# A hybrid decoder layer: where the last stage's weights are split, and how the S5 tables and the S5 scan are spread

## The chip, the core and the metric

The kernel runs on one core of a Trainium2 chip, in one launch. The metric is the device time in microseconds (us) from start to end. The core has a matrix engine (TensorE, PE in the profile; the loads of its stationary operand are PEld), three engines for elementwise work (VectorE = DVE, ScalarE = ACT, GpSimd = POOL) and SyncE (SP), which here issues the DMAs. Each engine works off its own instructions in the order in which the program holds them, and waits on semaphores for the others.

## The reference, cut to what matters

One layer over 2048 tokens of width 1024, in float32:

```
h = rms_norm(x);  proj = h @ w_in                        # 1024 -> 8716 columns
u_a, z_a, q, k, v, z_b, xbc, dt, z_c, gate_logits = split(proj)
y_a = s5_mixer(u_a, ...) * silu(z_a)                     # 32 diagonal complex state spaces, then a GLU
y_b = attention_mixer(q, k, v) * silu(z_b)               # 12 heads, windows (128,1) (512,4) (2048,16)
y_c = ssd_mixer(xbc, dt, z_c, ...)                       # conv, chunked scan, gated norm
g0, g1, g2 = sigmoid(gate_logits)
merged = g0 * (y_a @ proj_a) + g1 * (y_b @ proj_b) + g2 * (y_c @ proj_c)
out = x + merged @ w_out
```

Two pieces of it do not depend on x: the tables of the S5 scan (powers and phases of its complex decays, its B and C matrices multiplied out), and the weights proj_a, proj_b, proj_c and w_out themselves.

## The kernel before

Each large product is made of three matmuls: both operands are split into a high part and the rest (hi, lo; in code `wh`, `wl`), and hi*hi, hi*lo and lo*hi are added up. So every weight is first copied by ACT to its high part and then subtracted by DVE to its low part.

The main line is the input projection, in two halves of 1024 tokens. For each half the columns are taken in groups of 256, and a group takes four units. The first half's order is q, k, v and z_b of the attention (units 1 to 40), dt and z_c (41 to 52), xbc (53 to 72), u_a and z_a, called uz (73 to 88), and the gates (89 to 136); the second half's is uz (137 to 152), q, k, v (153 to 192), dt and z_c, xbc, gates (to 272). For each group `wload` brings 1 MB of weights into one buffer (`wr`), and `wsplit` (L361) splits it in four quarters (L368 on ACT, L369 on DVE); there are six buffers for high and six for low quarters, so that two quarters of the next group are split early and the other two only when TensorE has left the first quarters of the present one. TensorE's results stand in three PSUM banks (`mmps`) and are taken out by ACT.

Beside the main line run jobs, written as generators. `main` gives each a number of steps and a first and last unit between which its steps are spread evenly; what a step emits is then ordered on each engine by a scheduler that works with its own estimates before the program ever runs, so that a job's instructions often stand ahead of the unit in which they were emitted. The jobs that matter here:

- `s5_setup` (units 2 to 38) makes small S5 values, nearly all on DVE.
- `s5_tables` (40 steps): for each of eight blocks, products on POOL (L1060, L1061, L1104, L1105), adds on DVE, four transposes and four small matmuls on TensorE, and stores.
- `ssd` for the first half's chunks: decay matrices on POOL (L814) and matmuls on TensorE.
- `a0_early` (8 steps) norms the eight token tiles 8 to 15 of the second half: ACT squares, POOL takes the inverse root of the mean (L245, L246; tile `xs`), DVE multiplies x (L289), and TensorE transposes it (L295, tile `xT`).
- `out_weights` (20 steps) reads proj_a, proj_b, proj_c and w_out, splits them and stores them for the last stage (`pw_d`, `wo_d`). A step is one slab of 128 x 1024: a load into `ow`, ACT's copy (L1240) and DVE's subtraction (L1241) into `owh`, and two stores. Both tiles have two buffers.
- `s5` (42 steps) is the scan, `s5_glu` (25 steps) what follows it; then the second half's attention, its scan, and `final`, the last stage.

All DMAs named here stand in SP's one queue. Jobs take their tiles from pools that are opened and closed one after the other in the same memory.

Of the kernel before, what the change touches and what calls it, by code (L numbers as in the profile page):

```python
# [10 lines left out]
F32 = mybir.dt.float32  # L11
F32R = mybir.dt.float32r
BF16 = mybir.dt.bfloat16
I32 = mybir.dt.int32
AF = mybir.ActivationFunctionType
ALU = mybir.AluOpType
# [4 lines left out]
D = 1024  # L21
P = 128
# [5 lines left out]
NEG = -1.0e30  # L28
TABW = 162
ATTEND = 256  # L30
S5END = 196


class Small:
# [115 lines left out]
class Hybrid:  # L150
# [1074 lines left out]
    def out_weights(self):  # L1225

        nc, A = self.nc, self.A
        for j in range(20):
            if j < 4:
                src, k, scale = A["proj_a"], j, 0.125  # L1230
            elif j < 6:
                src, k, scale = A["proj_b"], j - 4, 0.5
            elif j < 12:
                src, k, scale = A["proj_c"], j - 6, self.snw[:, j - 6:j - 5]
            else:
                src, k, scale = A["w_out"], j - 12, 0.5
            raw = self.ct(f"ow{j}", [P, D], tag="ow", bufs=2)
            nc.sync.dma_start(raw, src[0, k * P:(k + 1) * P, :])
            hl = self.ct(f"owh{j}", [P, 2, D], F32R, tag="owh", bufs=2)
            nc.scalar.activation(hl[:, 0], raw, AF.Copy, scale=scale)  # L1240
            nc.vector.scalar_tensor_tensor(hl[:, 1], raw, scale, hl[:, 0].bitcast(F32),  # L1241
                                           op0=ALU.mult, op1=ALU.subtract)
            for x in range(2):
                if j < 12:
                    dst = self.pw_d[:, :, x, j, :].rearrange("t p c -> p t c")
                    nc.sync.dma_start(dst, hl[:, x].bitcast(F32).rearrange("p (t c) -> p t c", c=P))
                else:
                    dst = self.wo_d[:, :, x, j - 12, :].rearrange("t p c -> p t c")
                    nc.sync.dma_start(dst, hl[:, x].bitcast(F32).rearrange("p (t c) -> p t c", c=256))
            yield  # L1250

    def load_y(self, tb):
# [89 lines left out]
    def main(self):  # L1342
# [6 lines left out]
        def early(gen, n):  # L1349
            for _ in range(n):  # L1350
                yield next(gen)
# [20 lines left out]
        def open_pool(name):  # L1372
            st = ExitStack()
            return st, st.enter_context(self.tc.tile_pool(name=name, bufs=1, side="right"))

        def run(jobs, until):

            nonlocal u
            adv = steps(jobs)
            while u < until:  # L1380
                if next(units, 0) is None:
                    u += 1
                    adv(u)
                else:
                    break
            adv(10 ** 6)
# [9 lines left out]

        u, units = 0, all_units()
        st, self.jp = open_pool("jp0")
        run([(self.s5_setup(), 18, 2, 38)], 40)
        st.close()  # L1400
        s1, self.sp = open_pool("sp0")
        s2, self.jp = open_pool("jp1")
        ssd0, early0 = self.ssd(0), self.a0_early()
        run([(early(ssd0, 10), 10, 73, 82), (chain(self.attention(0, 0), self.attention(1, 0)), 40, 41, 80)], 82)
        s2.close()
        s2, self.jp = open_pool("jp1t")
        run([(early(ssd0, 36), 36, 83, 116), (self.s5_tables(), 40, 83, 115), (early0, 8, 84, 115)], 116)
        s2.close()
        s2, self.jp = open_pool("jp1w")
        run([(ssd0, 20, 117, 135), (self.out_weights(), 20, 117, 134)], 136)  # L1410
        s2.close()
        s1.close()
        st, self.jp = open_pool("jp2")
        run([(self.s5(), 42, 153, 180)], 180)
        st.close()
        st, self.jp = open_pool("jp2g")
        run([(self.s5_glu(), 25, 181, S5END)], S5END)
        st.close()
        self.late = [None, None]
        self.late[0], self.sp = open_pool("sp1")  # L1420
# [58 lines left out]
```

## Time and profile before

| | |
|---|---|
| median of 3 runs | 2519.76 us (2518.63 to 2520.58) |
| the profiled execution | 2518.61 us, its span 2516.5 us |
| TensorE busy | 2453.7 us, 98% of the span |
| VectorE, ScalarE, GpSimd busy | 1336.7, 783.9, 708.7 us |
| mean granted clock of TensorE | 0.986 |

The span is the time from the first to the last instruction; 2.1 us of the execution lie outside it. A matmul's row in the profile is longer than the time until the next one starts, since matmuls overlap; TensorE counts as busy while any of them runs. The clock is given as a share of the full 2.4 GHz, and it has two levels here, 1.00 and 0.50.

### The profile page before, as it was taken

To read this page: it belongs to the slowest core of one execution; us is meant where nothing else is said; L and a number is where in the kernel's file an instruction comes from. 1 tells how busy PE (TensorE), PEld (TensorE's weight loads), DVE (VectorE), ACT (ScalarE), POOL (GpSimd) and SP (SyncE) were. 2 spreads that over 40 slices of the span, in tenths; PEclk is the share of its full clock that TensorE was granted. 3 is DMA by queue.
4 is the path that set the end of the run, shared out by engine and by line. 5 is a ranking of instruction groups with operands and counts; after the bars stand their busy time and mean duration, and the time that the engine had idled before them with its cause. 6 is when DMAs were issued, how large, how long until landed. Compare 5 with 4: busy or idle time off the path is not lost.

```text
span 2516.5 us, 40172 instructions
## 1 busy us (share of the span) xinstructions
PE 2453.7 (98%) x15216; PEld 2158.3 (86%) x15216; DVE 1336.7 (53%) x2852; ACT 783.9 (31%) x1656; POOL 708.7 (28%) x737
## 2 busy tenths in 40 slices
PE   8999999999999999999999999999999899999999
PEld 8999988887777888899999988888887688888888
DVE  6942545538666443277765545632334767563321
ACT  4222344432223434222244244533332312121100
POOL 2221000029887330054442000000111455432120
PEclk8999999999999999999999999999999999999999
DMA  7433333435555997556554333433333789887886
GB/s 169 128 107 98 104 103 101 154 87 181 176 181 178 335 355 233 139 144 173 174 165 152 127 106 92 148 124 128 112 126 112 227 303 308 290 286 264 306 290 223
DMA packets 417088, 453.41 MB, mean 180 GB/s; under 512 B 103040, under 2 KB 358272, under 8 KB 409728
## 3 DMA queue, kind: packets, MB, share of 16 engines
q1 hardware_dynamic: 416896, 450.86, 56.2%
q8 instruction: 120, 1.97, 0.3%
q14 instruction: 72, 0.59, 0.1%
HBM read 304.80 MB, written 145.97 MB: 179 GB/s over the span
## 4 chain that ended last, share of the span: by engine, by line
PE 55%; DMA 6%; DVE 5%; POOL 4%; SPq 2%; issue 1%; ACT 1%; DVEq 0%; ACTq 0%; POOLq 0%
PE ps_g L392 5%; PE ps_g L394 5%; PE ps_g L393 5%; PE fp L1300 3%; PE fp L1302 3%; PE fp L1301 3%; PE op L1333 2%; PE op L1331 2%; PE op L1332 2%; PE ao L688 2%; PE ps_xbc L393 2%; PE ps_xbc L394 1%; PE ps_xbc L392 1%; PE as L659 1%; PE ps_uz L394 1%
## 5 line engine op out<-in xcount | busy, mean ns | idle before, releaser
L392 PE MATMUL ps_g<-hT_hi,wh_g 128*128 128x512 f32 x768 | 308.8, 402 | 1.6 <-DVE e_uz L466 1.1
L393 PE MATMUL ps_g<-hT_lo,wh_g 128*128 128x512 f32 x768 | 306.7, 399 | 0.0
L394 PE MATMUL ps_g<-hT_hi,wl_g 128*128 128x512 f32 x768 | 306.0, 398 | 0.0
L814 POOL TENSOR_TENSOR sr<-tle,ahl 128x384 fp32r<-128x384 f32 x128 | 122.1, 977 | 440.0 <-PE sd L819 305.9
L392 PEld LDWEIGHTS ps_g<-hT_hi,wh_g 128*128 128x128 f32 x768 | 144.8, 188 | 35.2 <-DVE e_uz L466 2.0
L394 PEld LDWEIGHTS ps_g<-hT_hi,wl_g 128*128 128x128 f32 x768 | 144.9, 189 | 33.5 <-issue 0.5
L393 PEld LDWEIGHTS ps_g<-hT_lo,wh_g 128*128 128x128 f32 x768 | 145.0, 189 | 32.7 <-issue 1.0
L1300 PE MATMUL fp<-fy_hi,fp 128*128 128x512 f32 x384 | 154.3, 402 | 0.5 <-DVE fg L1303 0.5
L1333 PE MATMUL op<-fo,fm_lo 128*128 128x256 f32 x512 | 146.3, 287 | 7.2 <-DVE fm_lo L1313 7.2
L1331 PE MATMUL op<-fo,fm_hi 128*128 128x256 f32 x512 | 147.8, 289 | 4.9 <-DMA fo<-wo_d 2.8
L1302 PE MATMUL fp<-fy_hi,fp 128*128 128x512 f32 x384 | 151.3, 394 | 0.0
L1301 PE MATMUL fp<-fy_lo,fp 128*128 128x512 f32 x384 | 150.9, 393 | 0.0
L1332 PE MATMUL op<-fo,fm_hi 128*128 128x256 f32 x512 | 146.5, 286 | 0.0
L1305 POOL TENSOR_TENSOR fm<-fm,fg 128x512 f32<-128x512 f32 x64 | 85.5, 1336 | 206.6 <-DVE fg L1303 190.9
L667 ACT ACTIVATE sm<-sm,ml 128x256 f32<-128x256 f32 (+1 forms) x192 | 86.4, 451 | 137.9 <-DVE ml L665 111.1
L392 PE MATMUL ps_xbc<-hT_hi,wh_xbc 128*128 128x512 f32 x320 | 129.0, 403 | 0.0
L394 PE MATMUL ps_xbc<-hT_hi,wl_xbc 128*128 128x512 f32 x320 | 128.6, 402 | 0.0
L393 PE MATMUL ps_xbc<-hT_lo,wh_xbc 128*128 128x512 f32 x320 | 128.6, 402 | 0.0
L369 DVE TENSOR_TENSOR wl_g<-wr_g,wh_g 128x512 fp32r<-128x512 f32 x96 | 77.2, 826 | 92.2 <-ACT wh_g L368 91.9
L506 DVE SCALAR_TENSOR_TENSOR ac_cv<-xb_cv,convw,ac_cv 128x512 f32<-128x512 f32 x120 | 91.6, 764 | 49.1 <-ACT ac_cv L504 48.3
L383 PE MATMUL ps_q<-wh_q,hT_lo 128*128 128x256 f32 x384 | 109.9, 287 | 3.0 <-DVE hT_lo L325 3.0
L381 PE MATMUL ps_q<-wh_q,hT_hi 128*128 128x256 f32 x384 | 111.2, 291 | 0.3 <-ACT wh_q L368 0.3
(418 smaller groups left out, 6953.8 us busy)
## 6 DMA issues: line engine op xcount, KB each, us to landing
fp<-pw_d SPq DMA_DIRECT2D x32, 1536.0 KB, 6.8
fo<-wo_d SPq DMA_DIRECT2D x16, 2048.0 KB, 8.7
wr_g<-in_w_in_dram SPq DMA_DIRECT2D x24, 1024.0 KB, 5.4
g_d<-e_g SPq DMA_DIRECT2D x96, 256.0 KB, 2.9
fg<-g_d SPq DMA_DIRECT2D x96, 256.0 KB, 7.0
pw_d<-owh SPq DMA_DIRECT2D x24, 512.0 KB, 6.5
wr_xbc<-in_w_in_dram SPq DMA_DIRECT2D x10, 1024.0 KB, 5.4
x<-in_x_dram SPq DMA_DIRECT2D x32, 256.0 KB, 4.4
```

What stands on the lines that cost most here:

```text
L381: nc.tensor.matmul(ps, hi[:, t], wh, start=kt == 0, stop=False)
L383: nc.tensor.matmul(ps, lo[:, t], wh, start=False, stop=kt == KT - 1)
L392: nc.tensor.matmul(ps, wh, hi, start=kt == 0, stop=False)
L393: nc.tensor.matmul(ps, wh, lo, start=False, stop=False)
L394: nc.tensor.matmul(ps, wl, hi, start=False, stop=kt == KT - 1)
L814: nc.gpsimd.tensor_mul(r, self.tle.unsqueeze(1).to_broadcast([P, 3, P]), ahl[:, i, h0:h0 + 3].unsqueeze(2).to_broadcast([P, 3, P]))
L1300: nc.tensor.matmul(ps, W[k][0], yh[k], start=k == k0, stop=False)
L1301: nc.tensor.matmul(ps, W[k][0], yl[k], start=False, stop=False)
L1302: nc.tensor.matmul(ps, W[k][1], yh[k], start=False, stop=k == k1 - 1)
L1331: nc.tensor.matmul(ps, mh[k][:, t], W[k][0], start=k == 0, stop=False)
L1332: nc.tensor.matmul(ps, mh[k][:, t], W[k][1], start=False, stop=False)
L1333: nc.tensor.matmul(ps, mlo[k][:, t], W[k][0], start=False, stop=k == 7)
```

## The change

Three lines of numbers in `main` and one generator change.

- `out_weights` runs in units 23 to 40, in the pool of `s5_setup`, and no longer in the last third of the first half's gates. It handles each slab in two halves of 512 columns: two loads of 256 KB, two copies, two subtractions and four stores of 256 KB where there were one load, one copy, one subtraction and two stores, all of twice the size. Both tiles keep two buffers, now of half the size. The stores still put 512 bytes in a row for `pw_d` and 1 KB for `wo_d`.
- `s5_tables` has its 40 steps in units 83 to 135 where they had 83 to 115, and the 56 steps of `ssd` that remain run evenly through 83 to 135, where 36 ran to 116 and 20 from 117. One pool (`jp1t`) holds until unit 136, and `jp1w` is gone.
- `s5` gets units 153 to 184 for its 42 steps where it had 153 to 180, `s5_glu` 185 to 200 for 181 to 196, and the second half's attention begins at 202 for 198 and ends as before.

```diff
-S5END = 196
+S5END = 200
...
-            raw = self.ct(f"ow{j}", [P, D], tag="ow", bufs=2)
-            nc.sync.dma_start(raw, src[0, k * P:(k + 1) * P, :])
-            hl = self.ct(f"owh{j}", [P, 2, D], F32R, tag="owh", bufs=2)
...
+            for q in range(2):
+                raw = self.ct(f"ow{j}_{q}", [P, 512], tag="ow", bufs=2)
+                nc.sync.dma_start(raw, src[0, k * P:(k + 1) * P, q * 512:q * 512 + 512])
+                hl = self.ct(f"owh{j}_{q}", [P, 2, 512], F32R, tag="owh", bufs=2)
+                nc.scalar.activation(hl[:, 0], raw, AF.Copy, scale=scale)
+                nc.vector.scalar_tensor_tensor(hl[:, 1], raw, scale, hl[:, 0].bitcast(F32),
+                                               op0=ALU.mult, op1=ALU.subtract)
...
-        run([(self.s5_setup(), 18, 2, 38)], 40)
+        run([(self.s5_setup(), 18, 2, 38), (self.out_weights(), 20, 23, 40)], 40)
...
-        run([(early(ssd0, 36), 36, 83, 116), (self.s5_tables(), 40, 83, 115), (early0, 8, 84, 115)], 116)
-        s2.close()
-        s2, self.jp = open_pool("jp1w")
-        run([(ssd0, 20, 117, 135), (self.out_weights(), 20, 117, 134)], 136)
+        run([(ssd0, 56, 83, 135), (self.s5_tables(), 40, 83, 135), (early0, 8, 84, 115)], 136)
...
-        run([(self.s5(), 42, 153, 180)], 180)
+        run([(self.s5(), 42, 153, 184)], 184)
...
-        run([(self.s5_glu(), 25, 181, S5END)], S5END)
+        run([(self.s5_glu(), 25, 185, S5END)], S5END)
```

What the scheduler makes of it is seen in the built order of the instructions. On GpSimd, just ahead of the inverse root of the early token tile 10 (`xs10`, the third of the eight), before; `s5...` are products of the tables, `sx`, `sxd`, `sxdd`, `sr` and `ssd_state` belong to the scan of branch C:

```order
L836 TENSOR_TENSOR sx1_6646<-sx1_6646,sy1_1_7104 128x384
L1105 TENSOR_TENSOR s5wt3_1_7732<-s5t3_7497 128x512
L795 TENSOR_TENSOR sxd2_7213<-sx2_7203,dt0_5988 128x768
L1105 TENSOR_TENSOR s5wt3_1_7732<-s5t3_7497 128x512
L796 TENSOR_TENSOR sx2_7203<-sx2_7203,hpar_423 128x768
L798 TENSOR_TENSOR sxdd2_7216<-sxd2_7213,edc0_6119 128x768
L245 TENSOR_SCALAR sss1_7150<-sss1_7150 128x1
L246 TENSOR_TENSOR sss1_7150<-sss1_7150,nhalf_104 128x1
L1060 TENSOR_TENSOR s5k3_7512<-s5t3_7497 128x512
L1060 TENSOR_TENSOR s5o3_7605<-s5t3_7497 128x512
L245 TENSOR_SCALAR xs10_7260<-xs10_7260 128x1
L246 TENSOR_TENSOR xs10_7260<-xs10_7260,nhalf_104 128x1
```

And at the same place now:

```order
L843 TENSOR_TENSOR ssd_state_422<-ssd_state_422,edc0_6399 128x384
L836 TENSOR_TENSOR sx1_6926<-sx1_6926,sy1_1_7345 128x384
L1060 TENSOR_TENSOR s5k2_7873<-s5t2_7795 128x512
L795 TENSOR_TENSOR sxd2_7469<-sx2_7459,dt0_6268 128x768
L796 TENSOR_TENSOR sx2_7459<-sx2_7459,hpar_423 128x768
L798 TENSOR_TENSOR sxdd2_7472<-sxd2_7469,edc0_6399 128x768
L245 TENSOR_SCALAR sss1_7397<-sss1_7397 128x1
L246 TENSOR_TENSOR sss1_7397<-sss1_7397,nhalf_104 128x1
L245 TENSOR_SCALAR xs10_7483<-xs10_7483 128x1
L246 TENSOR_TENSOR xs10_7483<-xs10_7483,nhalf_104 128x1
```

The tables are in their third block there (the names end in 2) where they were at the end of the fourth.

On ScalarE in the first half's q, k, v stretch, where the third and fourth quarters of the second k group (`wh_k1`) are copied, before; `e_...` are results taken out of PSUM and `sq_...` their squares:

```order
L432 COPY e_q1_0_1_1539<-ps_q1_0_1_1490 128x512
L434 ACTIVATE sq_q1_0_1_1540<-e_q1_0_1_1539 128x512
L432 COPY e_q1_1_0_1622<-ps_q1_1_0_1573 128x512
L434 ACTIVATE sq_q1_1_0_1623<-e_q1_1_0_1622 128x512
L368 CAST wh_k1_0_2_1790<-wr_k1_0_1780 128x2x256
L368 CAST wh_k1_0_3_1794<-wr_k1_0_1780 128x2x256
L432 COPY e_q1_1_1_1681<-ps_q1_1_1_1632 128x512
```

And now:

```order
L432 COPY e_q1_0_1_1539<-ps_q1_0_1_1490 128x512
L434 ACTIVATE sq_q1_0_1_1540<-e_q1_0_1_1539 128x512
L1241 ACTIVATE owh8_0_2913<-ow8_0_2911,snw_430 128x512
L1241 ACTIVATE owh8_1_2920<-ow8_1_2918,snw_430 128x512
L432 COPY e_q1_1_0_1622<-ps_q1_1_0_1573 128x512
L434 ACTIVATE sq_q1_1_0_1623<-e_q1_1_0_1622 128x512
L1241 ACTIVATE owh9_0_2995<-ow9_0_2993,snw_430 128x512
L368 CAST wh_k1_0_2_1790<-wr_k1_0_1780 128x2x256
L1241 ACTIVATE owh9_1_3002<-ow9_1_3000,snw_430 128x512
L368 CAST wh_k1_0_3_1794<-wr_k1_0_1780 128x2x256
L432 COPY e_q1_1_1_1681<-ps_q1_1_1_1632 128x512
```

Copies of the last stage's weights stand between the main line's, one of them between two quarters of k. The 40 of them begin in the third unit and end ahead of the result of the 30th.

## Rows read from the trace of the kernel before

**Rows 1.** Stretches: length, busy PE PEld DVE ACT POOL, clock, DMA share, GB/s

```profile
60.00:255.00 195.00, 195.00 (x1653) 195.00 (x1652) 105.69 (x448) 53.84 (x91) 41.51 (x40) 1.00 0.37 111
...
560.00:820.00 260.00, 242.11 (x1123) 192.95 (x1122) 180.10 (x212) 75.67 (x160) 225.43 (x198) 0.95 0.55 176
820.00:976.50 156.50, 156.50 (x731) 128.03 (x730) 75.26 (x94) 63.94 (x102) 47.08 (x46) 1.00 0.98 319
976.50:1066.00 89.50, 89.50 (x391) 72.58 (x390) 23.88 (x32) 28.37 (x42) 0.13 (x2) 1.00 0.63 175
1066.00:1384.00 318.00, 308.56 (x2400) 301.17 (x2399) 219.50 (x352) 104.38 (x185) 126.20 (x149) 0.99 0.55 163
```

**Rows 2.** PE's waits, 560 to 820: total us, times, longest

```profile
PE xT L295 <- DVE x L289: 14.9, 7, 4.6
```

**Rows 3.** Timeline, PE: start us, us, instruction, idle before it and releaser

```profile
603.89 2.29 PE L295 MATMUL xT<-ident,x 128*128 128x128 f32 x8 [4.62 <-DVE x L289]
...
634.10 1.12 PE L295 MATMUL xT<-ident,x 128*128 128x128 f32 x4 [3.46 <-DVE x L289]
...
700.27 0.66 PE L295 MATMUL xT<-ident,x 128*128 128x128 f32 x4 [2.84 <-DVE x L289]
...
764.92 0.66 PE L295 MATMUL xT<-ident,x 128*128 128x128 f32 x4 [2.60 <-DVE x L289]
```

**Rows 4.** Timeline of GpSimd ahead of the first of these waits

```profile
597.67 2.11 POOL L245 TENSOR_SCALAR xs<-xs 128x1 f32<-128x1 f32 x1
599.86 2.06 POOL L1104 TENSOR_TENSOR s5w<-s5t 128x512 f32<-128x512 f32 x2
601.88 0.56 POOL L246 TENSOR_TENSOR xs<-xs,nhalf 128x1 f32<-128x1 f32 x1
```

**Rows 5.** Stretches of 6.8 us, columns as in rows 1

```profile
602.80:609.60 6.80, 5.60 (x20) 4.56 (x20) 5.85 (x5) 2.54 (x5) 6.80 (x6) 0.50 0.06 24
...
780.00:786.80 6.80, 6.80 (x31) 5.53 (x30) 6.32 (x7) 1.52 (x4) 6.34 (x5) 1.00 0.10 31
```

**Rows 6.** Groups on GpSimd, 560 to 820: busy us, mean ns, idle before

```profile
L1104 POOL TENSOR_TENSOR s5w<-s5t 128x512 f32<-128x512 f32 x32 | 41.5, 1317 | 0.1
...
L814 POOL TENSOR_TENSOR sr<-tle,ahl 128x384 fp32r<-128x384 f32 x32 | 32.4, 1034 | 6.8 <-PE sd L819 6.8
```

**Rows 7.** Instructions of one line: ns min/median/max, first and last start

```profile
L1104 POOL TENSOR_TENSOR s5w<-s5t x32: 1046/1374/1771, 563.9 to 773.7; 128x512 f32<-128x512 f32 x32
...
L369 DVE TENSOR_TENSOR wl_g<-wr_g,wh_g x28: 673/816/1956, 591.0 to 818.3; 128x512 fp32r<-128x512 f32 x28
...
L369 DVE TENSOR_TENSOR wl_v<-wr_v,wh_v x12: 670/684/693, 61.0 to 209.7; 128x512 fp32r<-128x512 f32 x12
```

**Rows 8.** Groups on ScalarE and VectorE, 820 to 976.5, columns as in rows 6

```profile
L1240 ACT ACTIVATE owh<-ow 128x1024 fp32r<-128x1024 f32 x14 | 14.8, 1061 | 30.9 <-DMA ow<-in_proj_a_dram 12.3 <-DMA ow<-in_w_out_dram 9.5 <-DMA ow<-in_proj_b_dram 7.1
...
L1241 DVE SCALAR_TENSOR_TENSOR owh<-ow,owh 128x1024 fp32r<-128x1024 f32 x14 | 17.4, 1247 | 28.8 <-ACT owh L1240 28.8
```

**Rows 9.** DMA issues, 826 to 950: KB each, median us to landing

```profile
pw_d<-owh SPq DMA_DIRECT2D x22, 512.0 KB, 6.5
...
g_d<-e_g SPq DMA_DIRECT2D x20, 256.0 KB, 6.2
```

**Rows 10.** DMA issues, 60 to 190, the same columns

```profile
q_d<-e_q SPq DMA_DIRECT2D x8, 256.0 KB, 2.2
```

**Rows 11.** Timeline of ScalarE and VectorE at the second k group

```profile
117.07 1.34 ACT L368 CAST wh_k<-wr_k 128x512 fp32r<-128x512 f32 x2 [2.28 <-PE ps_q L383]
119.22 0.59 ACT L432 COPY e_q<-ps_q 128x512 f32<-128x512 f32 x1 [0.81 <-PE ps_q L383]
...
119.14 0.68 DVE L369 TENSOR_TENSOR wl_k<-wr_k,wh_k 128x512 fp32r<-128x512 f32 x1
```

**Rows 12.** PE's waits, 1066 to 1384, columns as in rows 2

```profile
PE s5yp L1167 <- POOL s5r L1164: 5.4, 5, 1.8
PE s5gp L1216 <- DVE s5gl L1209: 3.6, 2, 2.6
```

More of the change, by code (lines that the diff above doesn't have):

```diff
@@ L1236, in out_weights @@
                 src, k, scale = A["w_out"], j - 12, 0.5
-            raw = self.ct(f"ow{j}", [P, D], tag="ow", bufs=2)
-            nc.sync.dma_start(raw, src[0, k * P:(k + 1) * P, :])
-            hl = self.ct(f"owh{j}", [P, 2, D], F32R, tag="owh", bufs=2)
[L1240 to L1249, printed above, removed]
+            for q in range(2):
[5 more added lines that the diff above has]
+                                               op0=ALU.mult, op1=ALU.subtract)
+                for x in range(2):
+                    if j < 12:
+                        d, c = self.pw_d[q * 4:q * 4 + 4, :, x, j, :], P
+                    else:
+                        d, c = self.wo_d[q * 2:q * 2 + 2, :, x, j - 12, :], 256
+                    nc.sync.dma_start(d.rearrange("t p c -> p t c"),
+                                      hl[:, x].bitcast(F32).rearrange("p (t c) -> p t c", c=c))
             yield
```

## The prediction

> **What bounds the kernel now.** I read the page's busy times first: TensorE works 2453.7 of 2516.5 us. So the change can give back only what TensorE idles or runs at the lower clock, and take away only by making it wait where it does not wait now. Then the stretches, cut where the main line changes and where the jobs begin and end [rows 1]. In the first half's q, k, v (60 to 255) TensorE is busy for all of 195.00 us at clock 1.00. From 560 to 820, where the tables run, it misses 17.9 us and the clock is 0.95 on the mean; GpSimd is busy for 225.43 of the 260 us. From 820 to 976.5, where the last stage's weights are split, TensorE misses nothing, though the DMA engines are 0.98 busy. From 1066 to 1384, with the S5 scan, it misses 9.4 us.
>
> Third the waits of the stretch that loses most: 14.9 of its 17.9 us are transposes of early token tiles, which wait for VectorE's product with x [rows 2]. Four of them make up 13.5 us, at 604, 634, 700 and 765 us: tiles 8, 9, 11 and 13 [rows 3]. VectorE is not the cause: GpSimd had the inverse root to do, took 2.11 us for its first instruction, did two products of the tables in between and came to the second at 601.88, two microseconds before TensorE went on [rows 4]. Fourth the clock: behind each of the four waits there are 6.8 us at 0.50; in the first of them TensorE gets through 20 matmuls where it does 31 elsewhere [rows 5]. I price such a piece at half its length, 3.4 us. So this stretch loses 14.9 us of waits and 4 x 3.4 = 13.6 us of clock, 28.5 us in all; that is the most that the spreading can win there.
>
> **The tables, spread.** What counts is how much GpSimd work and how much TensorE work the built order puts between one early tile and the next. GpSimd: 225.43 us for 198 instructions, 1.14 us each [rows 1]. TensorE: 0.229 us for a matmul of 512 columns (89.50 us for 391, nearly all of them such) and 0.16 us for any other (in 820 to 976.5, 24 units of 24 such matmuls leave 156.50 - 576 x 0.229 = 24.6 us for 155 others) [rows 1]. Before, from tile to tile (8 to 9, 9 to 10, and so on to 15) GpSimd has 25, 24, 26, 24, 26, 24 and 15 instructions, or 28.5, 27.4, 29.6, 27.4, 29.6, 27.4 and 17.1 us; TensorE has 22.1, 27.4, 26.6, 27.9, 26.8, 27.7 and 20.6 us. The excess is 6.4 us for tile 9, of which the slow clock behind tile 8 hides 3.4, so 3.0; then 0, 3.0 for tile 11, nothing, 2.8 for tile 13, nothing, nothing. The trace has 3.46, 2.84 and 2.60 us at these three [rows 3]. The count explains it, so I use it for the new order.
>
> Now GpSimd has 23, 14, 23, 15, 32, 13 and 30 instructions between the tiles: 26.2, 16.0, 26.2, 17.1, 36.5, 14.8 and 34.2 us; TensorE has 20.6, 24.2, 24.8, 28.2, 33.4, 19.0 and 35.2. The spreading is uneven: a block of tables still comes in one burst. The excess is 5.6 - 3.4 = 2.2 us for tile 9, up to 1.4 for tile 11 (GpSimd is far ahead one tile earlier; I take 0.5), 3.1 for tile 13, and none for 10, 12, 14 and 15. For tile 8 the burst that begins the tables stands in both orders: GpSimd has three instructions less ahead of it (3.4 us), but TensorE's transposes stand 13 matmuls earlier (3.0 us), so the 4.62 us stay. Together 10.4 us of waits for 14.9, and three pieces of slow clock for four: 4.5 + 3.4 = 7.9 us won.
>
> That keeps GpSimd's instructions as slow as they are. One shape of them takes 1046 ns at best and 1771 at worst, with a mean of 1317 [rows 6, 7]; a subtraction on VectorE that takes 684 to 693 in the q, k, v stretch goes up to 1956 beside the tables [rows 7]. If they all fell to the best, 0.8 of the mean, the 26.2 us for tile 9 would be 21.0 and the 36.5 for tile 13 29.2: only tile 8 would wait, and the win would be 10.3 + 10.2 = 20.5 us. At the other end nothing is won, if the waits only move. I take 9, near the count. The page "SBUF — State Buffer" of the Trainium skill (Who interferes with whom) says that VectorE and GpSimd share a pair of ports, and that a VectorE instruction with two SBUF inputs and a GpSimd instruction that reads SBUF shut each other out for a whole instruction. The spread of durations agrees with it [rows 7]; by it, fewer VectorE instructions beside each burst would bring the 20.5 us, and the adds that belong to the burst itself would keep the 7.9.
>
> **The weight split, moved.** Where it leaves, nothing is won: TensorE misses nothing there, although ScalarE stood 30.9 us waiting for the slabs [rows 1, 8]. Where it goes, it stands in queues that feed a TensorE without slack. A unit there is 48 matmuls at 195.00 / 1653 = 0.118 us, 5.67 us [rows 1]; the 40 half slabs lie over 27 units, 153 us, 7.65 us for a pair. They move 10.5 MB in and 21 MB out, 206 GB/s, to the 111 that are there [rows 1]: 317, just what the DMA engines moved at a share of 0.98. So landings will not be the 2.2 us of a 256 KB store today [rows 10] but up to the 6.2 us of one beside the split [rows 9]. Two buffers mean that a pair takes at least one copy (0.53 us, half of 1061 ns), one subtraction (0.62) [rows 8] and one landing: 3.4 to 7.4 us. Both are under 7.65, the second barely.
>
> What is queued behind a late half slab decides. ScalarE's copies of the third and fourth quarter now stand right behind such a copy. The old times at the second k group: ScalarE copies from 117.07 to 118.41, VectorE's last subtraction ends at 119.82 [rows 11], and the fourth quarter is needed 18 to 36 matmuls into the group (two sums are interleaved), 2.1 to 4.2 us behind its start, which is about 119.0 (the fourth unit's result is taken out at 119.22 [rows 11]). That leaves 1.3 to 3.4 us. Taking results out of PSUM has two units, 11 us, to spare, since there are three banks; a late load of the weights themselves I price at nothing, as its buffer is free once the group before is split. Eight groups begin in these 27 units: I take 0.4 us for each, 3 us, between 0 and 1.5 each, 12 us. VectorE gets 40 x 0.62 = 25 us more to its 105.69 of 195 [rows 1, 8], which costs nothing by itself unless it falls behind.
>
> **The S5 scan, stretched** over 32 units for 28. Its waits are 5.4 us for the result of GpSimd and 3.6 for the GLU's low part [rows 12]; a burst an eighth less dense may save an eighth or the whole of the first: 0 to 5 us, or cost a microsecond or two by a worse order. I take 1. Attention's 72 steps over 54 units for 58 are the same work in front of a TensorE that is the bound on the whole; nothing.
>
> **The sum**: 2518.61 (the profiled execution: span 2516.5 and 2.1 outside it) - 9 + 3 - 1 = 2511.6 us. The median of the runs is 1.15 us above the profiled one, so 2513 us. A difference of 0.2%, 5 us, is about what can be told from none.
>
> **The rivals.** First, the bursts run at the best durations and all waits but one go: -20.5 + 3 - 1, or 2501 us. For it speaks that VectorE also has less to do per microsecond; against it that each block of tables brings its own adds. Chance 0.17. Second, slower: the split's chain becomes the bound in the first half's q, k, v. The place is ScalarE's and VectorE's queues at each group's third and fourth quarter; it decides from the point where a pair needs over 7.65 us, that is, a landing over 6.5. At 7.4 us a pair takes 8.6, the 20 pairs are 19 us late, and some three of the eight stops are long enough for 3.4 us of slow clock: -9 + 29 - 1, 2539 us. For it: the estimated 317 GB/s, and ScalarE's long waits for slabs [rows 8]. Against it: the same work at 0.98 of the DMA engines cost TensorE nothing in the gates, and half slabs keep shorter queues. Chance 0.13. Third, no change: the waits move to other tiles or to other readers of GpSimd, or lesser delays of the split eat up the win; 2516 to 2523 us, somewhat more often slower than faster. Chance 0.25. My forecast, 2506 to 2516 us, keeps 0.45.
>
> Faster by over 0.2% (under 2514.7): the first rival and most of the forecast, 0.55. Within 0.2%: the rest of the forecast and most of the third rival, 0.25. Slower: the second rival and the third's tail, 0.20. The range runs from 2498, past the first rival, to 2528; what lies outside is mostly the second rival.
>
> **What would show it.** Right: in the table stretch waits of about 4.6, 2 and 3 us at tiles 8, 9 and 13, hardly any at 11, and a piece of half clock behind each of the three; GpSimd busy until nearly the end of the gates; in 60 to 255 a TensorE that misses 2 to 5 us, all at the start of a group, and stores of `pw_d` landing in 4 to 6 us. Wrong: tile 8 without a wait (the first burst would matter less than I think), GpSimd's products near 1050 ns (first rival), or a q, k, v stretch longer by over 10 us or with half clock in it (second rival).

## The result, and the profile after

The changed kernel takes 2534.55 us (median of 4 runs, 2531.67 to 2539.8) for 2519.61 (4 runs): it is slower, by a ratio of 1.0062 with a 95% interval of 1.0044 to 1.0079. The forecast was 2513 us, the range 2498 to 2528.

Where it went is seen by cutting both traces at the same points of the main line: the first half's q, k, v; u_a, z_a and gates (the tables' stretch); the second half's q, k, v (S5 scan); from there to the first product of the last stage; the last stage. These are windows of the kernel before, with the columns of [rows 1]:

```profile
14.50:255.20 240.70, 237.47 (x1978) 236.77 (x1979) 140.48 (x551) 76.27 (x143) 54.77 (x60) 0.98 0.43 116
493.30:976.50 483.20, 465.31 (x2217) 375.79 (x2216) 277.42 (x363) 164.68 (x322) 282.58 (x254) 0.97 0.66 212
1066.20:1384.30 318.10, 308.66 (x2402) 301.31 (x2401) 219.80 (x353) 104.59 (x186) 126.20 (x149) 0.99 0.55 163
1384.30:2003.30 619.00, 609.90 (x3631) 514.37 (x3629) 294.37 (x792) 230.06 (x577) 56.94 (x72) 0.99 0.40 129
2003.30:2516.50 513.20, 495.81 (x2962) 439.45 (x2961) 243.22 (x395) 70.19 (x132) 173.73 (x148) 0.99 0.82 282
```

And these the same five of the changed kernel:

```profile
14.10:270.40 256.30, 243.97 (x1978) 240.78 (x1979) 165.16 (x591) 98.26 (x183) 53.31 (x60) 0.97 0.81 232
508.50:979.20 470.70, 457.47 (x2216) 370.39 (x2215) 246.90 (x343) 145.51 (x302) 271.73 (x254) 0.99 0.48 150
1068.90:1377.10 308.20, 297.15 (x2306) 290.45 (x2305) 205.26 (x342) 95.60 (x171) 121.78 (x147) 0.98 0.53 156
1377.10:1999.60 622.50, 611.80 (x3672) 517.71 (x3671) 287.49 (x766) 231.23 (x573) 50.73 (x64) 0.99 0.40 125
1999.60:2533.10 533.50, 510.35 (x3014) 447.96 (x3014) 264.20 (x432) 79.04 (x150) 185.50 (x158) 0.98 0.82 283
```

The first is 15.6 us longer, the second 12.5 us shorter. The last three must be taken together, since TensorE's count (the first "x") shows work that moved: 96 instructions fewer in the third, 41 more in the fourth and 52 more in the last. Together they take 1464.2 us for 1450.3, 13.9 longer. The sum, 15.6 - 12.5 + 13.9 = 17.0, is the span's difference of 16.6 with the 0.4 us by which the first window begins earlier. The forecast had +3, -9 and -1.

**The tables, with waits as forecast.** TensorE's waits for early tiles in the changed kernel, the answer to [rows 3]:

```profile
614.76 0.52 PE L295 MATMUL xT<-ident,x 128*128 128x128 f32 x3 [3.27 <-DVE x L289]
...
640.62 0.55 PE L295 MATMUL xT<-ident,x 128*128 128x128 f32 x3 [1.49 <-DVE x L289]
...
760.79 0.63 PE L295 MATMUL xT<-ident,x 128*128 128x128 f32 x4 [3.07 <-DVE x L289]
```

They are tiles 8, 9 and 13, with 3.3, 1.5 and 3.1 us for the 4.6, 2.2 and 3.1 forecast, nothing at tile 11, and 1.2 us at tile 15, which wasn't forecast. GpSimd's products kept their pace: the 32 of L1104 have a median of 1375 ns for 1374 in [rows 7]. Two pieces of half clock are left of four, 3.4 and 6.8 us long, none behind tile 9. Of the 12.5 us, 4.7 are shorter stops (13.2 us missed for 17.9) and 7.7, priced at half as the prediction does it, the clock: TensorE works through 10.2 us at half clock for 25.5.

**The split.** In the first half's q, k, v TensorE now stops at the starts of the groups, where it never stopped before from the second group on [rows 1]. The two longest:

```profile
150.00 0.50 PE L381 MATMUL ps_v<-wh_v,hT_hi 128*128 128x256 f32 x2 [1.97 <-ACT wh_v L368]
...
201.61 0.50 PE L381 MATMUL ps_k<-wh_k,hT_hi 128*128 128x256 f32 x2 [2.40 <-ACT wh_k L368]
```

By the windows TensorE misses 12.3 us for 3.2, 9.1 more. Behind each of these two stops stands a piece of 3.4 us at half clock (the third figure from the right), in which a matmul starts every 0.21 us where it is every 0.12 behind it: about 3 us of loss for the two:

```profile
151.70:155.10 3.40, 3.40 (x18) 3.40 (x17) 2.64 (x15) 0.00 (x0) 1.16 (x2) 0.50 0.93 270
202.90:206.30 3.40, 3.40 (x19) 3.40 (x17) 1.27 (x3) 0.32 (x1) 1.83 (x2) 0.50 0.99 276
```

Where the other 3.5 us lie, no row here shows. ScalarE ahead of the stop at 201.61:

```profile
192.36 1.23 ACT L1241 ACTIVATE owh<-ow 128x512 fp32r<-128x512 f32 x2 [3.23 <-DMA ow<-in_w_out_dram]
193.49 0.57 ACT L432 COPY e_q<-ps_q 128x512 f32<-128x512 f32 x1
194.09 0.63 ACT L434 ACTIVATE sq_q<-e_q 128x512 f32<-128x512 f32 x1
199.78 1.26 ACT L1241 ACTIVATE owh<-ow 128x512 fp32r<-128x512 f32 x2 [5.06 <-DMA ow<-in_w_out_dram]
200.96 1.12 ACT L368 CAST wh_k<-wr_k 128x512 fp32r<-128x512 f32 x2
```

The k weights, whose third and fourth quarter L368 copies, had landed at 186.8; the two quarters stand behind two copies of half slabs, which waited 5.06 us for their load. SyncE, and VectorE's subtractions of the pair before, show why the load was late:

```profile
193.01 2.04 SPq L1249 DMA_DIRECT2D wo_d<-owh  x4
195.15 1.30 SPq L1239 DMA_DIRECT2D ow<-in_w_out_dram  x2
...
200.44 0.38 SPq L1249 DMA_DIRECT2D wo_d<-owh  x1
```

```profile
193.02 1.29 DVE L1242 SCALAR_TENSOR_TENSOR owh<-ow,owh 128x512 fp32r<-128x512 f32 x2 [3.05 <-ACT owh L1241]
```

The next loads stand behind the stores of the pair before. A pair is one turn of a ring: copies at 192.36, the first load buffer read out at 193.71 and the second at 194.31, stores issued until 195.05, loads until 196.45, and the next copies at 199.78, right behind the first landing (199.62). That is 7.42 us. Copy and subtraction take 1.4 us of it, the place behind the stores another 1.4, the landing 4.5. Over the whole split the 20 pairs take 8.5 us each on the mean, from 45.5 to 217.2 us, where the prediction had 7.65 us of time for each: on the mean a load is issued 2.0 us after its buffer is free and lands 4.9 us after that, and each of the 40 copies starts within 0.7 us of its landing. So the loads set the pace, and the copies wait for them.

**The last stage.** TensorE's waits from 1985 us on, the three largest, and its first product of the last stage:

```profile
PE syd L828 <- DVE sm L822: 10.1, 5, 5.1
PE fp L1301 <- DMA fp<-pw_d: 6.3, 1, 6.3
PE spt L859 <- DVE sx L853: 2.9, 1, 2.9
```

```profile
1999.62 0.76 PE L1301 MATMUL fp<-fy_hi,fp 128*128 128x512 f32 x1 [6.28 <-DMA fp<-pw_d]
```

Before, the first product waited for nothing. Between the last gate product and it TensorE then did 48 matmuls, nearly all of branch C's second scan; now it does 8 there, so nothing covers the loading of the first weights. The fourth window as a whole misses only 1.6 us more (10.7 for 9.1), since before the change a stop for VectorE stood in the same place:

```profile
1994.75 1.51 PE L828 MATMUL syd<-sxd,sm 128*128 128x64 f32 x6 [5.58 <-DVE sm L822]
```

The groups of that stretch now:

```profile
L828 PE MATMUL syd<-sxd,sm 128*128 128x64 f32 x6 | 0.9, 283 | 1.2 <-DVE sm L822 1.2
L725 PE MATMUL mp<-ident,my 128*128 128x128 f32 x2 | 0.7, 434 | 1.6 <-DVE my L722 1.6
```

And more of that scan lies in the last stage: 144 products L828 for 122, 48 of L819 for 40.

What the 13.9 us of the last three windows consist of can be read off. TensorE misses 44.9 us for 35.9, 9.0 more, of which 5.8 in the last stage. It works through 29.4 us at half clock for 22.8, which priced at half are 3.3 us more. The longest piece begins among the stops ahead of the last stage, and the first products run in it, one every 0.43 us for 0.23 before:

```profile
1991.50:2005.10 13.60, 6.14 (x16) 4.53 (x17) 10.11 (x21) 1.41 (x4) 6.17 (x6) 0.50 0.90 330
```

Without stops and half clock the three windows take 1404.6 us for 1403.0. So the loss is in the stops and the clock behind them, and not in more work for TensorE.

### The profile page after: what moved, and what is told of

Read it like the earlier page. It is cut to its first block, busy times and chain, and to the rows that moved or that the text cites. A ratio compares the mean times of both kernels' runs of the same rounds, so it can differ in the third digit from the quotient of the medians.

```text
span 2533.1 us, 40326 instructions
## 1 busy us (share of the span) xinstructions
PE 2456.6 (97%) x15216; PEld 2156.8 (85%) x15216; DVE 1330.2 (53%) x2872; ACT 787.9 (31%) x1676; POOL 697.1 (28%) x737
## 4 chain that ended last, share of the span: by engine, by line
PE 71%; DMA 6%; DVE 6%; POOL 5%; issue 2%; ACT 1%; SPq 1%; DVEq 0%; ACTq 0%; POOLq 0%
PE ps_g L394 6%; PE ps_g L392 6%; PE ps_g L393 6%; PE fp L1301 3%; PE fp L1303 3%; PE fp L1302 3%; PE ps_xbc L392 3%; PE ps_xbc L394 3%; PE ps_xbc L393 3%; PE ao L688 3%; PE op L1332 2%; PE op L1333 2%; PE op L1334 2%; PE as L659 2%; PE ps_uz L392 2%
## 5 line engine op out<-in xcount | busy, mean ns | idle before, releaser
L369 DVE TENSOR_TENSOR wl_g<-wr_g,wh_g 128x512 fp32r<-128x512 f32 x96 | 76.2, 811 | 94.1 <-ACT wh_g L368 91.3
L381 PE MATMUL ps_k<-wh_k,hT_hi 128*128 128x256 f32 x384 | 111.2, 291 | 3.7 <-ACT wh_k L368 3.2
L571 ACT ACTIVATE e_g<-ps_g 128x512 f32<-128x512 f32 x96 | 56.9, 598 | 185.8 <-PE ps_g L394 176.8
```

The source lines that it names most:

```text
L381: nc.tensor.matmul(ps, hi[:, t], wh, start=kt == 0, stop=False)
```

## The experiments

All were timed in five rounds beside the kernel before on the same chip; ratios are to it. Single runs of the kernel before lay between 2512 and 2530 us there, which the intervals take in. Lengths of stretches are those of one profiled run each. How far they scatter is seen from kernels that have a stretch alike: the first half's q, k, v takes 240.5 to 242.0 us in six without the split, 251.4 to 256.3 in three with the change's split; the tables' stretch 483.0 to 484.6 in seven with the old tables, 470.5 to 477.1 in nine with the spread ones; the last stage 506.4 to 514.2 in seven with the old attention. "Changed" is the changed kernel; S5 "old" is units 153 to 180, GLU to 196 and attention from 198.

### The parts alone

**S5 later alone** (the kernel before):

```diff
-S5END = 196
+S5END = 200
...
-        run([(self.s5(), 42, 153, 180)], 180)
+        run([(self.s5(), 42, 153, 184)], 184)
...
-        run([(self.s5_glu(), 25, 181, S5END)], S5END)
+        run([(self.s5_glu(), 25, 185, S5END)], S5END)
```

> The kernel before with only the S5 scan in units 153 to 184, the GLU in 185 to 200 and the attention from 202. Theory: the later S5 pushes work of the attention and of the scan of branch C past the gates into the last stage, and that alone is the 20 us by which the last stage is longer in the changed kernel: 1.6 us more loss in the S5 stretch, some 13 in the last stage, 2530 to 2538 us, the last stage near 528 us. Rival: the last stage is longer for another reason (the order or the layout that comes with the other two edits); then 2517 to 2523 us and a last stage near 510 us.

2534.37 us, 1.0058 (1.0042 to 1.0075). The last stage is 536.3 us long, for "near 528" in the theory. This part alone costs about as much as the whole change; the rival falls.

**The split alone** (the changed kernel with tables and S5 as before):

```diff
-S5END = 200
+S5END = 196
...
-        run([(ssd0, 56, 83, 135), (self.s5_tables(), 40, 83, 135), (early0, 8, 84, 115)], 136)
+        run([(early(ssd0, 36), 36, 83, 116), (self.s5_tables(), 40, 83, 115), (early0, 8, 84, 115)], 116)
+        s2.close()
+        s2, self.jp = open_pool("jp1w")
+        run([(ssd0, 20, 117, 135)], 136)
...
-        run([(self.s5(), 42, 153, 184)], 184)
+        run([(self.s5(), 42, 153, 180)], 180)
...
-        run([(self.s5_glu(), 25, 185, S5END)], S5END)
+        run([(self.s5_glu(), 25, 181, S5END)], S5END)
```

> The kernel before with only the weight split moved to the first half's q, k, v, in half slabs; tables, scan of branch C and S5 as before. Theory: the q, k, v stretch is as long as in the changed kernel, about 256 us for 241, and nothing else moves: 2533 to 2537 us. Rival: the stretch is longer only together with the other edits, 2518 to 2523 us; or the last stage also gets longer, 2543 to 2550 us.

2526.17 us, 1.0017 (1.0002 to 1.0032), between the two theories. The q, k, v stretch is 253.6 us, as long as in the changed kernel within 3 us; the last stage was 506.4 us in this profile, the shortest of the seven, and that hides part of it.

**Split and tables** (changed, S5 old):

```diff
-S5END = 200
+S5END = 196
...
-        run([(self.s5(), 42, 153, 184)], 184)
+        run([(self.s5(), 42, 153, 180)], 180)
...
-        run([(self.s5_glu(), 25, 185, S5END)], S5END)
+        run([(self.s5_glu(), 25, 181, S5END)], S5END)
```

> The changed kernel with the S5 scan, GLU and attention back in their old units. Theory (the parts add up): 15.6 us lost in q, k, v, 12.4 won in the u_a, z_a and gate stretch, the last stage as before: 2521 to 2526 us. Rival (the last stage's loss comes from the other edits): 2531 to 2538 us. The difference to the kernel with the split alone is what the spreading of the tables is worth: theory 10 to 14 us.

2521.01 us, 1.0001 (0.9989 to 1.0013), as the sum of the parts has it. The q, k, v stretch takes 251.4 us, that of the tables 475.3 for 484.6 in the split alone. So the spreading is worth 9.3 us in its stretch, and the medians of the two differ by 5.2; the theory's 10 to 14 is missed, and the intervals of the two overlap. That the stretch is shorter is clear all the same, from the sixteen kernels above.

### What holds up the q, k, v stretch

**The split on GpSimd** (changed, S5 old), so that ScalarE and VectorE hold none of it:

```diff
-                nc.scalar.activation(hl[:, 0], raw, AF.Copy, scale=scale)
-                nc.vector.scalar_tensor_tensor(hl[:, 1], raw, scale, hl[:, 0].bitcast(F32),
-                                               op0=ALU.mult, op1=ALU.subtract)
+                if scale != 1.0:
+                    nc.gpsimd.tensor_scalar(raw, raw, scale, None, op0=ALU.mult)
+                nc.gpsimd.tensor_copy(hl[:, 0], raw)
+                nc.gpsimd.tensor_sub(hl[:, 1], raw, hl[:, 0].bitcast(F32))
```

> The changed kernel with S5 in its old units, and copy and subtraction of the last stage's weights on GpSimd (scaling, copy, subtraction), so that no waiting copy stands ahead of a weight quarter on ScalarE or VectorE. Theory: TensorE's waits at the group starts come from ScalarE's copies of the third and fourth quarter standing behind a copy that waits for its slab; the q, k, v stretch falls to 241 to 245 us and the kernel to 2508 to 2514 us. Rival: late weight loads behind the stores in SyncE's queue, or full DMA engines, make the wait; the stretch stays at 252 to 258 us and the kernel at 2520 to 2527 us.

2529.46 us, 1.0039 (1.0024 to 1.0055); the stretch stays at 252.4, as the rival had it, with a time above its range. Yet the rival's cause isn't what the trace shows: the stops no longer name ScalarE, but VectorE's low parts.

```profile
104.31 0.39 PE L382 MATMUL ps_q<-wl_q,hT_hi 128*128 128x256 f32 x1 [3.67 <-DVE wl_q L369]
```

VectorE had not waited; it was behind with its own queue, the small instructions of the S5 setup among them, which it did slowly. VectorE and GpSimd, ten microseconds ahead:

```profile
94.59 0.60 DVE L1030 TENSOR_SCALAR sm<-sm 128x32 f32<-128x32 f32 x1
95.23 0.19 DVE L1031 TENSOR_TENSOR sm<-sm,sm 128x32 f32<-128x32 f32 x1
95.34 1.28 DVE L1032 TENSOR_TENSOR sm<-sm,sm 128x32 f32<-128x32 f32 x1
96.54 0.18 DVE L908 TENSOR_TENSOR sm<-sm 128x32 f32<-128x32 f32 x1
```

```profile
94.36 0.80 POOL L1243 CAST owh<-ow 128x512 fp32r<-128x512 f32 x1
95.25 1.33 POOL L1244 TENSOR_TENSOR owh<-ow,owh 128x512 fp32r<-128x512 f32 x1
```

L1032 takes 1.28 us, where the same line takes 0.18 to 0.19 a few microseconds later, and ends within 0.05 us of GpSimd's subtraction. The run didn't test what it was made for; it moved the delay to the other engine that prepares a quarter. And the split, which ends at 217 us in the changed kernel, lasts until 326 here, so the stretch behind (dt, z_c and xbc) takes 244.7 us for 238.0:

```profile
266.90:511.60 244.70, 240.26 (x1579) 209.18 (x1578) 131.92 (x372) 101.25 (x239) 46.25 (x64) 0.99 0.47 145
```

**More buffers** (changed, S5 old): four buffers for the loads, or three for the loads and three for the split halves.

```diff
-                raw = self.ct(f"ow{j}_{q}", [P, 512], tag="ow", bufs=2)
+                raw = self.ct(f"ow{j}_{q}", [P, 512], tag="ow", bufs=3)
...
-                hl = self.ct(f"owh{j}_{q}", [P, 2, 512], F32R, tag="owh", bufs=2)
+                hl = self.ct(f"owh{j}_{q}", [P, 2, 512], F32R, tag="owh", bufs=3)
```

> The changed kernel with S5 in its old units and four buffers for the half slabs that are loaded, where it has two; the split halves keep two. Theory: ScalarE's copies wait for the slabs since with half slabs only two times 256 KB are under way where there were two times 512 KB; with four the loads are there, TensorE's waits at the group starts fall by more than half, the q, k, v stretch goes from 251 us to 242 to 247 us, the kernel to 2510 to 2517 us. Rival: the wait is for SyncE's queue, for the stores, or for full DMA engines; the stretch stays at 249 to 256 us, the kernel at 2518 to 2525 us.

> The same with three buffers for the loaded and three for the split half slabs. Theory: a copy waits for whichever of load and store is late; both have a third more time, so the stretch is 242 to 247 us and at least as short as with four and two, the kernel 2510 to 2517 us. If only the loads decide it stands between two and four load buffers; if neither, 249 to 256 us and 2518 to 2525 us.

Four and two: 2515.07 us, 0.9983 (0.9972 to 0.9995), the stretch 249.8; the time is as the theory had it, the stretch as the rival, and hardly shorter than with two and two. Three and three: 2507.23 us, 0.9961 (0.9946 to 0.9977), 3 us better than its range; the stretch 245.2, its row below, and 244.1 to 245.6 in the six kernels that have it. What ScalarE's copies wait for, from 40 to 270 us, says why: with two and two (split and tables) these rows,

```profile
ACT owh L1241 <- DMA ow<-in_w_out_dram: 33.7, 10, 7.2
ACT owh L1241 <- DMA ow<-in_proj_a_dram: 12.0, 5, 4.2
ACT owh L1241 <- DMA ow<-in_proj_c_dram: 9.1, 5, 2.9
```

with four loads the stores have taken their place,

```profile
ACT owh L1241 <- DMA pw_d<-owh: 22.2, 11, 3.4
ACT owh L1241 <- DMA ow<-in_w_out_dram: 3.7, 2, 3.1
```

and with three and three the stores and `w_out` are mostly gone, while the first slabs, of `proj_a`, wait as before.

```profile
ACT owh L1241 <- DMA ow<-in_proj_a_dram: 12.7, 5, 5.1
ACT owh L1241 <- DMA ow<-in_proj_c_dram: 3.9, 3, 2.1
```

```profile
14.60:259.80 245.20, 239.39 (x1979) 237.62 (x1980) 165.07 (x591) 99.66 (x183) 57.52 (x60) 0.98 0.83 242
```

The DMA engines move no less (242 GB/s for 236 in split and tables), and SyncE issues the same DMAs. A pair takes 7.5 us on the mean, under the 7.65, for 8.5 with two and two. So the ring of few buffers made the delay, not the rate of the DMA engines. Of 10.7 us against the stretch before, 6.2 go with one more buffer of each kind. By its ratio the kernel wins 10 us; the rest lies in the tables' stretch (472.5 for 475.3) and the last stage (510.3 for 513.4), which differ by as much among kernels that have them alike.

### What the later attention costs

**Attention from 202 alone** (the kernel before, one number):

```diff
-        ... 72, S5END + 2, ATTEND),
+        ... 72, S5END + 6, ATTEND),
```

> The kernel before with one number changed: the second half's attention begins in unit 202 for 198; S5 scan, GLU, split and tables as before, and four units in which no job gives TensorE anything. Theory: what costs in the later S5 is not the scan but the attention that begins 29 us later, since attention and the scan of branch C behind it keep their pace and end later; the last stage gets one more chunk of that scan (7.3 us of TensorE work) and stalls for its first weights: 2531 to 2538 us, the last stage from its first product 530 to 538 us for 513. Rival: the stretched scan itself (its order or its waits) does it; then 2518 to 2523 us and a last stage of 511 to 516 us.

2533.82 us, 1.0061 (1.0045 to 1.0077), the last stage 536.3 us. The stretched scan is not needed for the loss; the attention's start, which the program sets by S5's end and which so moved by 4 units, accounts for all of it.

**And 14 steps of the scan from unit 230:**

```diff
-             (early(ssd, 12), 12, 236, ATTEND)], ATTEND)
+             (early(ssd, 14), 14, 230, ATTEND)], ATTEND)
```

> The kernel before with the attention from unit 202, as in the run with that one number changed, and 14 steps of branch C's second scan from unit 230 where there were 12 from 236. In the order of this kernel the stretch between the last gate product and the first product of the last stage again holds work of that scan, as it does before the change, where the later attention alone left three matmuls and two transposes there. Theory: that work covers the loading of the last stage's first weights, and the loss is the lost cover and one chunk of the scan moved into the last stage; the first product then waits under 1 us for 6.3 to 6.9, the last stage is back at 508 to 520 us, the kernel at 2517 to 2525 us. Rival: a later attention costs whatever stands there (the work is pushed into a part with other limits): 2528 to 2538 us.

2529.92 us, 1.0041 (1.0025 to 1.0057): in the rival's range, though 4 us under the run before, whose interval overlaps. The last stage is 523.4 us, and the first product no longer waits for its weights, but others do; its waits from 1985 us:

```profile
PE mp L725 <- DVE msc L714: 5.6, 1, 5.6
PE mp L725 <- DVE my L722: 5.0, 2, 4.2
PE fp L1300 <- DVE fg L1303: 4.0, 2, 2.1
PE fp L1300 <- DVE fm L1303: 3.3, 1, 3.3
```

L725 transposes the attention's merged result. So the lost cover is at most the smaller part; the merging of heads is late too.

**Attention from 202, ended by 248** (scan from 236 again):

```diff
-        ... 72, S5END + 6, ATTEND),
+        ... 72, S5END + 6, ATTEND - 8),
```

> The kernel before with the attention's 72 steps over units 202 to 248 for 198 to 256. In its order the last stage and what stands ahead of it are as in the kernel before, and the last attention product stands one main-line unit later (with the late start alone, four). Theory: the late end of attention is what costs (the scan of branch C and the merging of heads behind it come late into the last stage), not its late start; the last stage is back at 508 to 517 us, the kernel at 2516 to 2524 us. Rival: the late start costs by itself, or a denser attention costs as much in the main line: 2528 to 2538 us.

2538.18 us, 1.0070 (1.0051 to 1.0089). The theory was right on the last stage and wrong on the kernel. Windows of xbc, gates and last stage:

```profile
1470.20:1648.30 178.10, 176.25 (x1051) 144.76 (x1050) 99.43 (x255) 86.42 (x209) 7.77 (x21) 0.99 0.35 104
1648.30:2024.70 376.40, 363.60 (x1904) 293.37 (x1902) 152.45 (x439) 122.06 (x328) 43.04 (x46) 0.98 0.42 135
2024.70:2538.10 513.40, 496.48 (x2962) 441.03 (x2961) 241.07 (x394) 70.21 (x132) 173.62 (x148) 0.98 0.82 282
```

The last stage is back, with 2962 instructions and 513.4 us. But xbc and gates, 526.4 us before, take 554.5, although TensorE does only 113 instructions more there; it now misses 14.6 us for 9.1 and works through 16.8 us at half clock for 4.2. (The second half's q, k, v and dt ahead of them are 7.9 us shorter, with 127 instructions fewer.) So the late start itself costs, and where it is paid depends on where the attention's work is put.

**S5 earlier** (the kernel before):

```diff
-S5END = 196
+S5END = 192
...
-        run([(self.s5(), 42, 153, 180)], 180)
+        run([(self.s5(), 42, 153, 176)], 176)
...
-        run([(self.s5_glu(), 25, 181, S5END)], S5END)
+        run([(self.s5_glu(), 25, 177, S5END)], S5END)
```

> The kernel before with the S5 scan in units 153 to 176, GLU in 177 to 192 and attention from 194: the same shift the other way. In its order the last attention product stands one main-line unit earlier than before. Theory: attention's end moves with it by about a unit, 7 us, and no whole chunk of the scan of branch C leaves the last stage, so it wins 0 to 5 us there and loses 0 to 4 us by a denser S5: 2515 to 2522 us. Rival: the effect is even on both sides, 12 us less by four units earlier, 2506 to 2511 us.

2516.91 us, 0.9989 (0.9978 to 1.0000): faster by at most a few microseconds, if at all. The effect is one-sided, as the theory had it.

### Put together

**Changed, with three and three buffers only** (the two lines of the diff above):

> The changed kernel with one thing different, three buffers for each of the two tiles of half slabs; S5 and attention stay late. Theory (losses add up by stretch): the q, k, v stretch 244 to 247 us, the tables' win kept, the last stage still near 530 us: 2517 to 2524 us, so two thirds of the loss against the changed kernel goes and the rest is the late attention. Rival: the kernel is not the sum of its stretches, 2506 to 2513 us or over 2528.

2525.94 us, 1.0018 (1.0006 to 1.0030), the q, k, v stretch 244.8, the last stage 536.3. The first is as forecast, the second 6 us above "near 530"; the time is 2 us above its range.

**The same, with attention ended by 248:**

```diff
-        ... 72, S5END + 2, ATTEND),
+        ... 72, S5END + 2, ATTEND - 8),
```

> The changed kernel with two things different: three buffers for each tile of half slabs, and attention's steps in units 202 to 248 for 202 to 256. Theory: both losses of the change are then taken away and the win at the tables stays: 2504 to 2511 us, the same as with S5 in its old units. Rival: attention keeps part of its loss in this order, 2515 to 2526 us.

2525.69 us, 1.0021 (1.0007 to 1.0035): the rival, nothing is won by the earlier end.

**Three and three with S5 old, and one more edit each:**

```diff
-... (early0, 8, 84, 115)], 136)
+... (early0, 8, 84, 131)], 136)
```

```diff
-S5END = 196
+S5END = 192
```

```diff
-        ... 72, S5END + 2, ATTEND),
+        ... 72, S5END + 2, ATTEND - 8),
```

> Three and three buffers, S5 in its old units, and the eight early token tiles over units 84 to 131 for 84 to 115. By the count of the prediction GpSimd then has 16 to 32 instructions between two tiles (18 to 36 us) and TensorE 32 to 42 us, so only tile 8 should wait: about 3 us of waits for 9.7, one piece of half clock for three, 6 to 9 us less than with three and three alone, 2498 to 2503 us. Rival: the waits go with the bursts of the tables and turn up elsewhere, 2504 to 2511 us.

> Three and three buffers, the S5 scan in its old units, the GLU in 181 to 192 for 181 to 196, attention from unit 194. In the order the second half's attention begins four main-line units earlier and ends one earlier. Theory: as with the S5 scan four units earlier, attention's earlier start wins little, since the cover of the last stage is already there; a denser GLU loses a microsecond or two: 2503 to 2509 us. Rival: the last stage shortens as it grew in the other direction, 2494 to 2499 us.

> Three and three buffers, S5 in its old units, and attention in units 198 to 248 for 198 to 256; its last product stands three units earlier than before. Theory: the cover of the last stage was there already, so an earlier end wins little, 2501 to 2508 us. Rival: the last stage shortens by as much as a later end lengthened it, 2492 to 2498 us, or a denser attention costs more than it gives, 2509 to 2516 us.

2507.39 (0.9953, 0.9938 to 0.9968), 2507.49 (0.9956, 0.9940 to 0.9972) and 2506.14 us (0.9947, 0.9928 to 0.9966): none can be told from three and three alone. The last of them tells something of the late attention: it has the 72 steps over 50 units, denser than the 54 of the change, and loses nothing, so with the old start a denser attention doesn't cost. The first was forecast to win 6 to 9 us by the count of instructions between tiles, and didn't: tile 8 waits as forecast, but so does tile 9, and all waits for early tiles together are 9.8 us for 10.3.

```profile
602.73 1.64 PE L295 MATMUL xT<-ident,x 128*128 128x128 f32 x5 [3.21 <-DVE x L289]
...
643.48 0.44 PE L295 MATMUL xT<-ident,x 128*128 128x128 f32 x1 [3.11 <-DVE x L289]
```

So the version to keep is the split moved and the tables spread, with three and three buffers and S5 in its old units: 0.39% or 10 us faster than the kernel before by its ratio, where the changed one is 0.62% slower.

## Why the prediction was wrong, point by point

**The tables: right mechanism, and a size with some luck in it.** 9 us were taken, near the 7.9 counted from GpSimd's and TensorE's instructions between tiles; 12.5 were measured in the whole change and 9.3 beside the same split. The three tiles named are those with the longest waits, and shorter stops gave 4.7 us for the 4.5 counted. The clock gave 7.7 us for 3.4, since tile 9's wait has no half clock behind it and tile 8's only 3.4 us; beside the same split it gave 1.8 us, and the stops 6.8. Of the signs, one didn't come: GpSimd isn't busy until nearly the end of the gates (13 of 40 us from 900 to 940). Spreading the early tiles further did not follow the same count, so that count holds for these two orders and not as a rule.

**The split: right mechanism, wrong size.** The prediction put the delay at the groups' third and fourth quarters, in ScalarE's queue behind a late half slab, and priced it at 3 us, 0 to 12. It was 15.6. The sentence that failed is "I take 0.4 us for each". It came from the slack of one quarter, and from a pair that was priced as copy, subtraction and one landing, "Both are under 7.65", with the loads free of the stores. In the trace the loads stand behind the stores in SyncE's queue and go out 2.0 us after their buffer is free, on the mean; so a pair takes 8.5 us, over the 7.65, with loads that land in 4.9 us, not 6.2. Nineteen turns at 0.9 us too much are 17 us, near what the stretch lost. The second rival named this place and the 7.65 us, and its sign came (a stretch longer by over 10 us, with half clock in it); but it put the cause in a landing over 6.5 us, and priced some three stops with slow clock where there were two. Its other argument, that half slabs keep queues short, looks the wrong way round: with two buffers each, half slabs halve what is under way, and a third buffer of each kind helped. That the old place in the gates bore the waits of ScalarE [rows 8] because whole slabs had twice as much under way is argued only; whole slabs were not tried in the new place, nor was a change of the order of loads and stores.

**S5 and attention: this step failed.** "Attention's 72 steps over 54 units for 58 are the same work in front of a TensorE that is the bound on the whole; nothing." The S5 scan itself was a small matter, though not the gain of 1 us: its waits for GpSimd are 7.9 us for the 5.4 of [rows 12], and S5 later costs no more than the later attention alone. But the attention's start was tied to S5's end, and its 4 units later cost 15 us by themselves (attention from 202, by its ratio); S5 and attention together cost 13.9 in the change. The work is the same, as the prediction had it; but TensorE stands still for longer around it. The trace of before gave the warning: TensorE misses 17.4 of 513.2 us in the last stage and 9.1 in the fourth window, so it is not the only bound there. The prediction cut its windows at 1384 us and looked at nothing behind. Nor did it read the built order there, which shows the lost cover ahead of the first product.

**The sum.** -9 + 3 - 1 was forecast; -12.5 + 15.6 + 13.9 happened. By this sum each of the two misses alone would have left the time inside the range; both together are outside it, though the tables won 3.5 us more than forecast.

**What stays open.** Why four units fewer cost 10 to 18 us, by the ratios, in the four arrangements tried on the kernel before (S5 later, attention from 202, the same with the earlier scan, the same ended by 248). It is shown that the loss goes with the late start and not with a denser attention alone, that it can sit in the last stage or in xbc and gates, and that neither the lost cover nor the scan's extra chunk makes up all of it. From the second half's q, k, v to the end these four miss 9.5 to 13.8 us more than before and lose 1.3 to 6.8 us more to half clock; all else differs by under 3 us (half clock priced at half). It is not shown which wait of the attention sets the room that it needs.

## What to carry to other kernels

When a job's window moves, read every job whose start is written relative to it, and the program's end: here a number that delayed a neighbour cost as much as the whole change. Price a transfer ring by one full turn (compute, issues on the DMA queue, landing, for each buffer) against the time that there is for it, and count bytes under way before tiles are halved. An in-order engine that feeds the bounding engine should not hold an instruction that waits for memory without buffers enough that it doesn't wait.

## What the runs showed of the hardware

A VectorE instruction on 128x32 that takes 0.18 to 0.19 us took 1.28 beside GpSimd's subtraction, and ended with it. The page "SBUF — State Buffer" of the Trainium skill (Who interferes with whom) says that a VectorE instruction with two SBUF inputs and a GpSimd instruction that reads SBUF exclude each other for a whole instruction; this trace agrees. So a small instruction cost seven times its time here. Moving 120 instructions to GpSimd, 90 of them in the first half's q, k, v, freed ScalarE there (76.2 us busy for 98.8) and put VectorE behind, until TensorE waited 3.67 us for one of its weight quarters.

The first products of the last stage waited 6.28 us for a load that nothing covered; and the issue of a 256 KB DMA held SyncE's queue for 0.51 to 0.65 us each (four stores in 2.04 us, two loads in 1.30), 3.3 us for the six of a pair, so that loads behind stores went out 1.4 us after their first buffer was free in the turn shown.
